# A transformer step on one core: the first scale and shift in pieces of one feature tile, products of zeros in TensorE's waits, and the last sums in another order

## The chip, the core and the metric

The kernel runs on one core of a Trainium2 chip. Its engines take their instructions in the order in which they are written: TensorE (PE; its weight loads are shown as PEld), VectorE (DVE), ScalarE (ACT), GpSimd (POOL) and SyncE (SP), which issues the transfers. The metric is the device time of one execution in microseconds, the median of several runs.

## The reference

Two layers act on 128 context tokens and 256 latent tokens of 1024 features. Each layer is a SwiGLU half step, a block of three mixers (gated short convolution, neighbourhood attention, latent attention), and a second SwiGLU half step. Ahead of each, a normalised x is scaled and shifted by vectors that come from the condition through `w_ada`:

```python
mod_ctx = (jax.nn.silu(c_ctx) @ w_ada[l] + b_ada[l]).reshape(1, 1, N_MOD, D_MODEL)
mod_lat = (jax.nn.silu(c) @ w_ada[l] + b_ada[l]).reshape(-1, 1, N_MOD, D_MODEL)
h = modulate(rmsnorm(x, ng[0]), m(0), m(1))        # h * (1 + scale) + shift
x = x + 0.5 * m(2) * swiglu(h, p['w_ffn1_gate'], p['w_ffn1_up'], p['w_ffn1_down'])
y_prompt = rmsnorm(xp, final_g)
```

The first scale and shift (m(1) and m(0) of layer 0) are needed by the very first products of the kernel; the last `rmsnorm` is its end.

## The kernel before

**Layout.** All 384 tokens lie together, features on partitions: X is eight feature tiles of 128 x 384. Every dense product is three TensorE products, since operand and weight are split into hi and lo parts: hi x hi, lo x hi, hi x lo (`mm3`). The weights come in the order of their use as chunks of 512 KB (`wst`), each eight blocks of 128 x 128. A dense chunk lands in one of three buffers raw; ScalarE writes its hi (line 320), VectorE its lo (line 321), and then the buffer is free for the next chunk (`Weights.split`, `release`, `pump`). The text calls the dense chunks d0, d1, d2 and so on. All these transfers are issued by SP, in the order of the program; one that needs a buffer waits on SP for it, and all behind it wait too. SP also waits for the transfer issued eight before.

**The start.** `first_group` makes six output tiles at once (three of the gate, three of the up projection of FFN 1), over the feature tiles k = 0 to 7; per k six groups (j = 0 to 5) of three products of 386 columns, with 48 blocks, chunks d0 to d5. The first scale and shift are not ready then. Sixteen chunks s0 to s15 of `w_ada` bring them, four at a time for a quarter of the features (two tiles). `start_quarter` multiplies the condition cz with a chunk (products of 256 columns in four column groups of the array), VectorE copies the partial sums (line 402), and `finish` transposes them and adds the four parts (lines 407, 408), adds the bias and then `scales` and `scaled` (lines 506 to 518) write hh and hl, the scaled X of the two tiles. `add_square` collects the squares of X; once all are there, 1/rms is computed by three newton steps on VectorE over 128 x 384 (`inverse_rms`, lines 432 to 451), into rb. The outputs of the first group are multiplied by rb afterwards; for all later products the eight tiles are normalised properly (`norm_tile`: line 524 on VectorE, 527 and 367 on ScalarE, 368 on VectorE), a few steps of it after each k as the table START_STEPS says.

**What follows.** `pair(f)`, f = 3 to 21, makes the other gate and up tiles (line 661), sixteen blocks each: k = 0 to 3 from one chunk, k = 4 to 7 from the next. pair(3) uses d6 and d7. The rest of the kernel is dense products one behind the other.

**The end.** X is transposed back (line 1008), the squares are summed by products with a column of ones (`rms_sums`, line 462): acc holds the tiles 0 to 6, w the last one. Three newton steps follow on VectorE, and then the scaling and the three last transfers.

Of the kernel before, what the change touches and what calls it, by code (L numbers as in the profile page):

```python
# [49 lines left out]
START_STEPS = {4: (0, 1, 0, 2, 1, 0), 5: (3, 2, 1, 4, 3, 2), 6: (5, 4, 3, 6, 5, 4), 7: (7, 6, 5, 7, 6, 7)}  # L50


START = {0: 0, 1: 1, 3: 2, 5: 3}
# [9 lines left out]
def plan():  # L63
# [3 lines left out]
    items = [("ahead", 1)]  # L67
# [11 lines left out]
    def ffn(l, n):  # L79
        g, u, dn = (f"w_ffn{1 + n // 2}_{x}" for x in ("gate", "up", "down"))  # L80
        start = (l, n) == (0, 0)
        for k in range(KD):
            if start and k in START:
                items.extend(("s", 0, m, START[k], i) for m in (1, 0) for i in range(2))
            for f in range(GROUP // 2):
                blk(g, l, k, slice(f * P, f * P + P))
                blk(u, l, k, slice(f * P, f * P + P))
# [111 lines left out]
def pack(inputs):  # L199
    order = chunks()  # L200
    out = np.empty((len(order), P, BPC * P), np.float32)
    for i, c in enumerate(order):
# [3 lines left out]
        elif c[0] == "s":  # L206
            at = c[2] * D + c[3] * 2 * P
            w = inputs["w_ada"][c[1], c[4] * D // 2:(c[4] + 1) * D // 2, at:at + 2 * P]
            out[i].reshape(P, 4, 2 * P)[:] = w.reshape(4, P, 2 * P).transpose(1, 0, 2)
# [66 lines left out]
class Weights:  # L276
# [3 lines left out]
    def __init__(self, nc, pool, src):  # L280
# [10 lines left out]
        self.ahead = 1  # L291
# [53 lines left out]
def step_kernel(ctx, tc, xT, cc, wst, cst_d, vec_d, rpb, ck_na, cv_na, ck_kv, ck_r, yd, o_k, o_v, o_ckv, o_kr):  # L345
# [36 lines left out]
    mods = [base.tile([P, NMOD, KD, 2], F32, name=f"mod{l}") for l in range(L)]  # L382
    hh = base.tile([P, KD, TOK + 2], F32R, name="hh")
# [7 lines left out]
    def start_quarter(m, c, cz):  # L391

        acc = ps()
        for half in range(2):
            i, what, raw = W.ada()
            assert what == ("s", 0, m, c, half), (what, m, c, half)
            w = raw.rearrange("p (k n) -> p k n", k=4)
            for j in range(4):
                nc.tensor.matmul(acc[32 * j:32 * j + 32, 0:2 * P], cz[:, 4 * half + j, :], w[:, j, :],
                                 start=half == 0, stop=half == 1)  # L400
        t = wt(2 * P)
        nc.vector.tensor_copy(t, acc[:, 0:2 * P])

        def finish():
            tp = ps()
            for i in range(2):
                nc.tensor.transpose(tp[:, i * P:(i + 1) * P], t[:, i * P:(i + 1) * P], ident)
            nc.vector.tensor_reduce(mods[0][:, m, 2 * c:2 * c + 2, :],
                                    tp[:, 0:2 * P].rearrange("p (i j v) -> p i v j", i=2, j=4)[:, :, 0:2, :],
                                    axis=AX.X, op=ALU.add)  # L410
            add_bias(0, m, 2 * c, 2)
# [646 lines left out]
```

## Time and profile before

| | |
|---|---|
| median of 3 runs | 1905.04 us (1904.65 to 1905.15) |
| profiled execution | 1904.49 us, its span 1902.7 us |
| TensorE busy | 1875.3 us, 99% of the span |
| VectorE, ScalarE busy | 1312.3 us, 813.2 us |
| transfers | 306.12 MB, mean 161 GB/s |

The span is the time from the first to the last instruction that the profiler saw. Times in the rows below count from the span's start. A row of a timeline merges equal instructions that follow one another and gives how many; what stands in brackets is the idle time of the engine before them, and the event that ended it.

### The profile page before, as it was taken

Reading aid. Unit: us, or ns where it says so; the run is one execution under the profiler, and the core shown is the slowest. Engines: PE = TensorE matmul, PEld = TensorE weight load, DVE = VectorE, ACT = ScalarE, POOL = GpSimd, SP = SyncE. Lnnn points to the kernel's source line nnn. Section 1 sums busy time; section 2 is a strip of 40 time slices with the busy share of each in tenths; the row PEclk is TensorE's granted clock in tenths of the full one; section 3 lists DMA queues with packets and bytes.
Section 4 is the critical chain, followed back from the end, with each engine's and each line's share of the span. In section 5 each row is a group of like instructions: output and inputs, shape, how many; then the busy total and the mean of one; then the engine's idle time right before and its main releaser. Section 6 shows DMA issues by size and latency. Waiting matters only on the chain.

```text
span 1902.7 us, 27717 instructions
## 1 busy us (share of the span) xinstructions
PE 1875.3 (99%) x10804; PEld 1824.2 (96%) x10804; DVE 1312.3 (69%) x2235; ACT 813.2 (43%) x1358; POOL 45.1 (2%) x79
## 2 busy tenths in 40 slices
PE   6999999999999999999999999999999999999998
PEld 5999999988999999999999999998789999999997
DVE  6788767665877778776778776666578766744433
ACT  4633334655533354333354333356554334633332
POOL 0000000013000000000000000000220000000000
PEclk9999999999999999999999999999999999999999
DMA  7567554423455535655535664533335643343331
GB/s 304 190 230 227 198 178 151 130 79 111 144 191 174 196 106 181 219 198 188 178 122 195 206 207 169 186 108 118 101 100 175 205 163 122 112 140 122 127 125 63
DMA packets 85523, 306.12 MB, mean 161 GB/s; under 512 B 9616, under 2 KB 11248, under 8 KB 85264
## 3 DMA queue, kind: packets, MB, share of 16 engines
q1 hardware_dynamic: 83376, 297.21, 46.8%
q0 software_dynamic: 1728, 5.41, 1.0%
q8 instruction: 84, 1.38, 0.3%
q10 hardware_dynamic: 288, 1.74, 0.3%
q14 instruction: 47, 0.39, 0.1%
HBM read 301.53 MB, written 2.79 MB: 160 GB/s over the span
## 4 chain that ended last, share of the span: by engine, by line
PE 93%; DVE 3%; ACT 2%; issue 1%; DMA 0%; SPq 0%; DVEq 0%; ACTq 0%
PE ps L661 34%; PE ps L363 18%; PE ps L362 18%; PE ps L364 18%; PE ps L874 1%; PE ps L911 1%; PE ps L927 1%; PE ps L820 1%; PE ps L818 1%; PE ps L819 1%; ACT w L527 1%; ACT prob L895 0%; DVE lo L321 0%; DVE small L889 0%; ACT hi L320 0%
## 5 line engine op out<-in xcount | busy, mean ns | idle before, releaser
L321 DVE TENSOR_TENSOR lo<-raw,hi 128x1024 fp32r<-128x1024 f32 x414 | 504.8, 1223 | 245.6 <-ACT hi L320 243.9
L320 ACT CAST hi<-raw 128x1024 fp32r<-128x1024 f32 x414 | 429.7, 1046 | 361.6 <-PE ps L363 230.8
L362 PE MATMUL ps<-hh,hi 128*128 128x384 f32 (+1 forms) x960 | 327.4, 341 | 1.9 <-ACT hh L516 1.4
L363 PE MATMUL ps<-hl,hi 128*128 128x384 f32 (+1 forms) x960 | 326.5, 340 | 2.4 <-DVE hl L368 1.8
L364 PE MATMUL ps<-hh,lo 128*128 128x384 f32 (+1 forms) x960 | 325.9, 339 | 0.0
L424 DVE SCALAR_TENSOR_TENSOR junk<-rawa,cb 128x1024 bf16<-128x1024 f32 x256 | 312.9, 1222 | 4.4
L661 PE MATMUL ps<-hl,hi 128*128 128x384 f32 x1216 | 312.6, 338 | 0.0
L661 PE MATMUL ps<-hh,lo 128*128 128x384 f32 x1216 | 312.1, 338 | 0.0
L661 PE MATMUL ps<-hh,hi 128*128 128x384 f32 x1216 | 310.3, 336 | 0.0
L364 PE MATMUL ps<-ah,lo 128*128 128x384 f32 x704 | 237.8, 338 | 0.0
L362 PE MATMUL ps<-ah,hi 128*128 128x384 f32 x704 | 237.8, 338 | 0.0
L363 PE MATMUL ps<-al,hi 128*128 128x384 f32 x704 | 237.8, 338 | 0.0
L661 PEld LDWEIGHTS ps<-hh,lo 128*128 128x128 f32 x1216 | 221.7, 188 | 0.0
L661 PEld LDWEIGHTS ps<-hh,hi 128*128 128x128 f32 x1216 | 221.3, 188 | 0.0
L661 PEld LDWEIGHTS ps<-hl,hi 128*128 128x128 f32 x1216 | 220.1, 188 | 0.0
L362 PEld LDWEIGHTS ps<-hh,hi 128*128 128x128 f32 x960 | 182.2, 190 | 5.5 <-ACT hh L516 1.8
L363 PEld LDWEIGHTS ps<-hl,hi 128*128 128x128 f32 x960 | 181.7, 189 | 3.6 <-DVE hl L368 2.3
L364 PEld LDWEIGHTS ps<-hh,lo 128*128 128x128 f32 x960 | 182.1, 190 | 0.0
L362 PEld LDWEIGHTS ps<-ah,hi 128*128 128x128 f32 x704 | 132.2, 188 | 0.0
L364 PEld LDWEIGHTS ps<-ah,lo 128*128 128x128 f32 x704 | 132.2, 188 | 0.0
L363 PEld LDWEIGHTS ps<-al,hi 128*128 128x128 f32 x704 | 132.2, 188 | 0.0
L638 ACT ACTIVATE w<-ps 128x384 f32<-128x384 f32 x76 | 37.2, 490 | 165.4 <-PE ps L661 165.4
(193 smaller groups left out, 1909.1 us busy)
## 6 DMA issues: line engine op xcount, KB each, us to landing
raw<-wst SPq DMA_DIRECT2D x414, 512.0 KB, 3.4
rawa<-wst SPq DMA_DIRECT2D x128, 512.0 KB, 3.4
s<-wst SPq DMA_DIRECT2D x16, 512.0 KB, 10.0
bias<-rpb POOLq DMA_DIRECT2D x16, 256.0 KB, 3.3
X<-xT SPq DMA_DIRECT2D x4, 384.0 KB, 9.5
y<-X SPq DMA_DIRECT2D x3, 512.0 KB, 3.9
cb<-cc ACTq DMA_DIRECT2D x1, 1024.0 KB, 6.8
cst<-cst ACTq DMA_DIRECT2D x1, 672.0 KB, 4.8
```

Source lines behind the costliest of these rows:

```text
L320: nc.scalar.copy(hi, raw)
L321: nc.vector.tensor_tensor(lo, raw, hi.bitcast(F32), op=ALU.subtract)
L362: nc.tensor.matmul(out, w[0], x[0], start=start, stop=False)
L363: nc.tensor.matmul(out, w[0], x[1], start=False, stop=False)
L364: nc.tensor.matmul(out, w[1], x[0], start=False, stop=stop)
L424: nc.vector.scalar_tensor_tensor(junk, w, 1.0, cb[:, v], op0=ALU.mult, op1=ALU.mult, accum_out=mods[l][:, m, t, v:v + 1])
L527: nc.scalar.activation(h[:, sl], h[:, sl], AF.Identity, bias=mods[l][:, 3 * idx, t, s:s + 1], scale=A[0][:, t, s:s + 1])
L638: nc.scalar.activation(s, g[:, :TOK], AF.Silu)
L661: nc.tensor.matmul(o[:, :TOK], w[part], y, start=k == 0 and i == 0, stop=k == KD - 1 and i == 2)
L818: nc.tensor.matmul(o, xh, wh, start=k == 0, stop=False)
L819: nc.tensor.matmul(o, xl, wh, start=False, stop=False)
L820: nc.tensor.matmul(o, xh, wl, start=False, stop=k == KD - 1)
```

## The change

It touches the first 60 us and the last 15 us of the kernel.

- The first scale and shift come in pieces of one feature tile. A chunk s now holds all 1024 rows of one tile's 128 columns, for scale or for shift; tile 0 needs s0 and s1, tile 1 s2 and s3, and then two tiles at a time (START). `start_tiles` takes the place of `start_quarter`: eight products of 128 columns for each chunk in place of four of 256.
- X is loaded in pieces: tile 0 behind s1, tile 1 at (k=0, j=2), tiles 2-3 at (k=1, j=0), the others at k=2. Before, two tiles each stood among the first chunks.
- At the start only one dense chunk is split ahead of tile 0's scale (`ahead` 0), the second behind tile 1's.
- `busy(n)` issues n products of a zero matrix, 128 x 512 in bf16: ten at the very start, four behind the products of s0 and s1, six behind tile 0's transposes, four behind the products of s2 and s3.
- The steps of `norm_tile` start at k=5 in place of k=4.
- At the end two tiles are transposed in place of four ahead of the sums, the three sums of acc stand ahead of those of w, and the two are added on VectorE.

```diff
--- before.py
+++ after.py
@@ -47,10 +47,12 @@
 STEPS = {2: (0, 1, 0, 2, 1, 0), 3: (3, 2, 1, 4, 3, 2), 4: (5, 4, 3, 6, 5, 4), 5: (7, 6, 5, 7), 6: (6,), 7: (7,)}
-START_STEPS = {4: (0, 1, 0, 2, 1, 0), 5: (3, 2, 1, 4, 3, 2), 6: (5, 4, 3, 6, 5, 4), 7: (7, 6, 5, 7, 6, 7)}
-START = {0: 0, 1: 1, 3: 2, 5: 3}
+START_STEPS = {5: (0, 1, 0, 2, 1, 0, 3), 6: (2, 1, 4, 3, 2, 5, 4, 3, 6), 7: (5, 4, 7, 6, 5, 7, 6, 7)}
+START = {(0, 0): ((0,), (0, 0)), (0, 2): ((1,), (0, 5)), (1, 0): ((2, 3), (1, 2)), (3, 0): ((4, 5), (3, 2)),
+         (5, 0): ((6, 7), (5, 2))}
 O_B, O_C, O_X = 0, 512, 1024
@@ -64,7 +66,7 @@
-    items = [("ahead", 1)]
+    items = [("ahead", 0)]
     def blk(name, l, k, cols):
         items.append(("d", name, l, k * P, cols))
@@ -80,9 +82,11 @@
         g, u, dn = (f"w_ffn{1 + n // 2}_{x}" for x in ("gate", "up", "down"))
         start = (l, n) == (0, 0)
         for k in range(KD):
-            if start and k in START:
-                items.extend(("s", 0, m, START[k], i) for m in (1, 0) for i in range(2))
             for f in range(GROUP // 2):
+                if start and (k, 2 * f) in START:
+                    items.extend(("s", 0, m, t) for t in START[k, 2 * f][0] for m in (1, 0))
+                    if f:
+                        items.append(("ahead", 1))
                 blk(g, l, k, slice(f * P, f * P + P))
                 blk(u, l, k, slice(f * P, f * P + P))
         if start:
@@ -204,9 +208,9 @@
             at = c[2] * D + c[3] * P
             out[i] = inputs["w_ada"][c[1], :, at:at + P].T
         elif c[0] == "s":
-            at = c[2] * D + c[3] * 2 * P
-            w = inputs["w_ada"][c[1], c[4] * D // 2:(c[4] + 1) * D // 2, at:at + 2 * P]
-            out[i].reshape(P, 4, 2 * P)[:] = w.reshape(4, P, 2 * P).transpose(1, 0, 2)
+            at = c[2] * D + c[3] * P
+            w = inputs["w_ada"][c[1], :, at:at + P]
+            out[i].reshape(P, KD, P)[:] = w.reshape(KD, P, P).transpose(1, 0, 2)
         else:
             for b, (_, name, l, r, cols) in enumerate(c[1]):
                 out[i, :, b * P:(b + 1) * P] = inputs[name][l][r:r + P, cols]
@@ -288,7 +292,7 @@
         self.parts = {}
         self.split_at = 0
         self.n = 0
-        self.ahead = 1
+        self.ahead = 0
     def pump(self, tag, upto=None):
         ring = self.rings[tag]
@@ -380,6 +384,7 @@
     nc.gpsimd.memset(up, 0.0)
     mods = [base.tile([P, NMOD, KD, 2], F32, name=f"mod{l}") for l in range(L)]
+    spool = []
     hh = base.tile([P, KD, TOK + 2], F32R, name="hh")
     hl = base.tile([P, KD, TOK + 2], F32R, name="hl")
@@ -388,27 +393,31 @@
         mod = mods[l][:, m, t:t + n, :]
         nc.vector.tensor_tensor(mod, mod, b.unsqueeze(2).to_broadcast([P, n, 2]), op=ALU.add)
-    def start_quarter(m, c, cz):
-        acc = ps()
-        for half in range(2):
-            i, what, raw = W.ada()
-            assert what == ("s", 0, m, c, half), (what, m, c, half)
-            w = raw.rearrange("p (k n) -> p k n", k=4)
-            for j in range(4):
-                nc.tensor.matmul(acc[32 * j:32 * j + 32, 0:2 * P], cz[:, 4 * half + j, :], w[:, j, :],
-                                 start=half == 0, stop=half == 1)
-        t = wt(2 * P)
-        nc.vector.tensor_copy(t, acc[:, 0:2 * P])
+    def start_tiles(ts, cz):
+        acc, n = ps(), len(ts)
+        for a, t in enumerate(ts):
+            for m in (1, 0):
+                i, what, raw = W.ada()
+                assert what == ("s", 0, m, t), (what, m, t)
+                w = raw.rearrange("p (k n) -> p k n", k=KD)
+                at = slice((n * m + a) * P, (n * m + a + 1) * P)
+                for k in range(KD):
+                    j = k % 4
+                    nc.tensor.matmul(acc[32 * j:32 * j + 32, at], cz[:, k, :], w[:, k, :], start=k < 4, stop=k >= 4)
+        x = spool[0].tile([P, 4 * P], F32, tag="st", bufs=2, name="st")[:, :2 * n * P]
+        nc.vector.tensor_copy(x, acc[:, :2 * n * P])
         def finish():
             tp = ps()
-            for i in range(2):
-                nc.tensor.transpose(tp[:, i * P:(i + 1) * P], t[:, i * P:(i + 1) * P], ident)
-            nc.vector.tensor_reduce(mods[0][:, m, 2 * c:2 * c + 2, :],
-                                    tp[:, 0:2 * P].rearrange("p (i j v) -> p i v j", i=2, j=4)[:, :, 0:2, :],
-                                    axis=AX.X, op=ALU.add)
-            add_bias(0, m, 2 * c, 2)
+            for i in range(2 * n):
+                nc.tensor.transpose(tp[:, i * P:(i + 1) * P], x[:, i * P:(i + 1) * P], ident)
+            for m in range(2):
+                nc.vector.tensor_reduce(mods[0][:, m, ts[0]:ts[0] + n, :],
+                                        tp[:, n * m * P:n * (m + 1) * P].rearrange(
+                                            "p (i j v) -> p i v j", i=n, j=4)[:, :, 0:2, :],
+                                        axis=AX.X, op=ALU.add)
+                add_bias(0, m, ts[0], n)
         return finish
@@ -542,29 +551,53 @@
             nc.vector.memset(cz, 0.0)
             nc.scalar.activation(cz[:, :, 0:2], vec[:, V_C:V_BADA].rearrange("p (k v) -> p k v", v=2), AF.Silu)
         rest = {}
-        def start(c):
-            for finish in rest.pop(c):
-                finish()
-            scales(0, 0, slice(2 * c, 2 * c + 2))
-            if c == 0:
+        if pool:
+            spool[:] = [pool]
+            warm = pool.tile([P, 512], BF16, name="warm")
+            nc.vector.memset(warm, 0.0)
+            def busy(n):
+                o = ps()
+                for _ in range(n):
+                    nc.tensor.matmul(o, warm[:, 0:P], warm, start=True, stop=True)
+            busy(10)
+        def start(ts, finish):
+            finish()
+            n = len(ts)
+            scales(0, 0, slice(ts[0], ts[0] + n))
+            if ts[0] == 0:
                 W.split(0)
-            for t in (2 * c, 2 * c + 1):
+            for t in ts:
                 scaled(t)
-            if c < 2:
-                add_square(2 * c)
-                add_square(2 * c + 1)
+            if ts[0] < 4:
+                for t in ts:
+                    add_square(t)
         out = [ps() for _ in range(GROUP)]
         for k in range(KD):
-            if pool and k in START:
-                rest[START[k]] = [start_quarter(m, START[k], cz) for m in (1, 0)]
-                if k == 0:
-                    start(0)
+            if pool and k == 2:
+                for t in (4, 6):
+                    nc.sync.dma_start(out=X[:, t:t + 2, :], in_=xT[:, t:t + 2, :])
             for j, o in enumerate(out):
-                if pool and k % 2 and k < KD - 1 and j == 2:
-                    W.prepare()
-                    start(k // 2 + 1)
+                if pool and (k, j) in START:
+                    ts, at = START[k, j]
+                    if 0 < ts[0] < 4:
+                        nc.sync.dma_start(out=X[:, ts[0]:ts[-1] + 1, :], in_=xT[:, ts[0]:ts[-1] + 1, :])
+                    rest[at] = ts, start_tiles(ts, cz)
+                    if k == 0:
+                        busy(4)
+                if pool and (k, j) in rest:
+                    if k and k < KD - 1:
+                        W.prepare()
+                    start(*rest.pop((k, j)))
+                    if (k, j) == (0, 0):
+                        busy(6)
+                    elif k == 0:
+                        W.ahead = 1
+                        W.split(1)
                 mm3(o[:, :TOK + 2], W.next(), (hh[:, k, :], hl[:, k, :]), k == 0, k == KD - 1)
             if pool and k == 2:
                 for t in range(4, KD):
@@ -619,9 +652,8 @@
         if start:
             with tc.tile_pool(name="start", bufs=1, reuse_waits="tile") as pool:
                 W.start = [pool.tile([P, BPC * P], F32, name=f"s{i}") for i in range(16)]
-                for t, upto in ((0, 5), (2, 10), (4, 12), (6, 16)):
-                    W.pump("raw", upto)
-                    nc.sync.dma_start(out=X[:, t:t + 2, :], in_=xT[:, t:t + 2, :])
+                W.pump("raw", 2)
+                nc.sync.dma_start(out=X[:, 0, :], in_=xT[:, 0, :])
                 W.pump("raw")
                 out, rb, b = first_group(l, idx, pool)
             W.ahead = AHEAD
@@ -1007,9 +1039,17 @@
                 o = out[i][t // 4][:, t % 4 * P:t % 4 * P + P]
                 nc.tensor.transpose(o, X[:, t, i * P:(i + 1) * P], ident)
-    turn(range(4))
-    [r] = rms_sums([(sumsq, D)])
-    turn(range(4, KD))
+    turn(range(2))
+    ss = ps()
+    for n, sq in enumerate(sumsq):
+        for i in range(3):
+            nc.tensor.matmul(ss[:, 3 * n + i:3 * n + i + 1], sq[:, i * P:(i + 1) * P], ones[:, 0:1],
+                             start=True, stop=True)
+    v0, v = small(3), small(3)
+    nc.vector.tensor_scalar(v0, ss[:, 0:3], 1.0 / D, EPS, op0=ALU.mult, op1=ALU.add)
+    nc.vector.scalar_tensor_tensor(v, ss[:, 3:6], 1.0 / D, v0, op0=ALU.mult, op1=ALU.add)
+    r = rsqrt(v, 3)
+    turn(range(2, KD))
     y = X.rearrange("p t c -> p (t c)").rearrange("p (i h c) -> p i h c", i=3, h=2)
     for i in range(3):
         nc.scalar.activation(y[:, i, 0, :], out[i][0], AF.Copy, scale=r[:, i:i + 1])
```

**SP around the first pieces of X.** Names: s4_84 is chunk s4, raw_100 the first dense chunk d0, raw_103 d1, raw_110 d2, raw_163 d3. Before:

```order
L304 DMA raw_100<-wst 128x1024
L624 DMA X_64<-xT 128x768
L304 DMA raw_103<-wst 128x1024 [waits DMAHW0_49]
L304 DMA s4_84<-wst 128x1024 [waits DMAHW1_49]
L304 DMA s5_85<-wst 128x1024 [waits DMAHW2_49]
L304 DMA s6_86<-wst 128x1024 [waits DMAHW3_49]
L304 DMA s7_87<-wst 128x1024 [waits DMAHW4_49]
L624 DMA X_64<-xT 128x768 [waits DMAHW5_49]
L304 DMA raw_110<-wst 128x1024 [waits DMAHW6_49]
L624 DMA X_64<-xT 128x768 [waits DMAHW7_49]
L624 DMA X_64<-xT 128x768 [waits DMAHW0_49]
L304 DMA raw_163<-wst 128x1024 [waits DMAHW1_49,DVE_49]
```

After, from d3 on (raw_172 is d3, raw_252 d4; ahead of it stand vec, cst, s0, s1, X tile 0, d0, s2, s3, d1, s4 to s7 and d2):

```order
L308 DMA raw_172<-wst 128x1024 [waits DMAHW6_49,DVE_49]
L308 DMA s8_88<-wst 128x1024 [waits DMAHW7_49]
L308 DMA s9_89<-wst 128x1024 [waits DMAHW0_49]
L308 DMA s10_90<-wst 128x1024 [waits DMAHW1_49]
L308 DMA s11_91<-wst 128x1024 [waits DMAHW2_49]
L588 DMA X_64<-xT 128x384 [waits DMAHW3_49]
L308 DMA raw_252<-wst 128x1024 [waits DMAHW4_49,DVE_49]
L308 DMA s12_92<-wst 128x1024 [waits DMAHW5_49]
L308 DMA s13_93<-wst 128x1024 [waits DMAHW6_49]
L308 DMA s14_94<-wst 128x1024 [waits DMAHW7_49]
L308 DMA s15_95<-wst 128x1024 [waits DMAHW0_49]
L588 DMA X_64<-xT 128x768 [waits DMAHW1_49]
```

X tile 1 (128x384) and X tiles 2-3 (128x768) moved behind s11 and s15; before, all of X stood ahead of s8. d4 stands between the two pieces.

**VectorE around the second dense chunk.** lo_183 and lo_249 are the lo part of d1. Before:

```order
L518 SCALAR_TENSOR_TENSOR hl_74<-X_64,A_155,hh_73 128x128
L518 SCALAR_TENSOR_TENSOR hl_74<-X_64,A_155,hh_73 128x256
L518 SCALAR_TENSOR_TENSOR hl_74<-X_64,A_155,hh_73 128x128
L518 SCALAR_TENSOR_TENSOR hl_74<-X_64,A_155,hh_73 128x256
L497 TENSOR_TENSOR acc_177<-acc_177,w_179 128x384
L321 TENSOR_TENSOR lo_183<-raw_103,hi_182 128x1024
```

VectorE after, at the same chunk; the two hl are those of tile 1:

```order
L527 SCALAR_TENSOR_TENSOR hl_74<-X_64,A_164,hh_73 128x128
L527 SCALAR_TENSOR_TENSOR hl_74<-X_64,A_164,hh_73 128x256
L506 TENSOR_TENSOR acc_182<-acc_182,w_245 128x384
L325 TENSOR_TENSOR lo_249<-raw_103,hi_248 128x1024
L409 COPY st_295<-ps_262 128x512
L325 TENSOR_TENSOR lo_304<-raw_109,hi_303 128x1024
```

d1's lo stood behind hl and the squares of the tiles 0 and 1, and stands now behind those of tile 1, whose X is a transfer of its own.

**VectorE behind the newton steps.** rb is 1/rms; w_426, w_428 and w_432 are the first three products of X with it, the copies bring the partial sums of s12 to s15. Before:

```order
L437 SCALAR_TENSOR_TENSOR rb_389<-w_388,rb_389 128x384
L321 TENSOR_TENSOR lo_403<-raw_186,hi_402 128x1024
L524 TENSOR_TENSOR w_426<-X_64,rb_389 128x384
L524 TENSOR_TENSOR w_428<-X_64,rb_389 128x384
L524 TENSOR_TENSOR w_432<-X_64,rb_389 128x384
L368 TENSOR_TENSOR hl_74<-w_426,hh_73 128x384
L402 COPY w_447<-ps_438 128x256
L402 COPY w_458<-ps_449 128x256
L321 TENSOR_TENSOR lo_467<-raw_242,hi_466 128x1024
```

VectorE after, from the last newton step on:

```order
L446 SCALAR_TENSOR_TENSOR rb_467<-w_466,rb_467 128x384
L325 TENSOR_TENSOR lo_481<-raw_252,hi_480 128x1024
L409 COPY st_537<-ps_504 128x512
L325 TENSOR_TENSOR lo_546<-raw_307,hi_545 128x1024
L416 TENSOR_REDUCE mod0_71<-ps_551 128x4
L394 TENSOR_TENSOR mod0_71<-mod0_71,vec_65 128x4
L416 TENSOR_REDUCE mod0_71<-ps_551 128x4
L394 TENSOR_TENSOR mod0_71<-mod0_71,vec_65 128x4
L515 SCALAR_TENSOR_TENSOR A_164<-mod0_71,vec_65 128x4
```

The products with rb moved from ahead of the copy to behind d5's lo (lo_546), the reduction and the hl of tiles 6 and 7.

## Rows read from the trace of the kernel before

**Rows 1.** The page's chain of what ended last: shares of the span by engine.

```profile
PE 93%; DVE 3%; ACT 2%; issue 1%; DMA 0%; SPq 0%; DVEq 0%; ACTq 0%
```

**Rows 2.** Windows: stretch, length, busy time by engine, granted clock, transfers' share, GB/s.

```profile
38.00:40.00 2.00, 2.00 (x29) 1.31 (x31) 1.87 (x4) 0.00 (x0) 0.00 (x0) 1.00 0.01 2
44.00:46.00 2.00, 0.00 (x0) 0.00 (x0) 0.89 (x2) 1.96 (x5) 0.00 (x0) 0.93 0.71 236
52.00:54.00 2.00, 2.00 (x11) 2.00 (x11) 1.56 (x3) 2.00 (x5) 0.00 (x0) 0.86 0.00 0
```

**Rows 3.** Timeline of TensorE: start, us, line, operation, count, idle before and releaser.

```profile
8.59 1.08 PE L399 MATMUL ps<-s,cz 128*32 128x256 f32 x8 [0.20 <-DMA s<-wst]
9.87 1.08 PE L399 MATMUL ps<-s,cz 128*32 128x256 f32 x8 [0.20 <-DMA s<-wst]
...
19.65 1.93 PE L399 MATMUL ps<-s,cz 128*32 128x256 f32 x32
...
22.68 0.60 PE L407 MATMUL ps<-cst,w 128*128 128x128 f32 x4
...
25.23 0.34 PE L362 MATMUL ps<-hh,hi 128*128 128x386 f32 x1
...
47.29 1.12 PE L407 MATMUL ps<-cst,w 128*128 128x128 f32 x4 [5.36 <-DVE w L402]
...
58.65 0.51 PE L661 MATMUL ps<-hh,hi 128*128 128x384 f32 x2
...
62.84 0.34 PE L661 MATMUL ps<-hh,hi 128*128 128x384 f32 x1
```

**Rows 4.** Timeline of ScalarE.

```profile
20.78 1.05 ACT L320 CAST hi<-raw 128x1024 fp32r<-128x1024 f32 x1 [4.82 <-DMA raw<-wst]
23.88 1.50 ACT L516 ACTIVATE hh<-X,A 128x128 fp32r<-128x128 f32 x4 [2.06 <-DVE A L506]
25.28 0.93 ACT L493 ACTIVATE w<-X 128x384 f32<-128x384 f32 x2
...
56.14 0.99 ACT L527 ACTIVATE w<-w,mod,A 128x128 f32<-128x128 f32 x2 [0.46 <-DVE w L524]
...
57.44 0.99 ACT L527 ACTIVATE w<-w,mod,A 128x128 f32<-128x128 f32 x2
```

**Rows 5.** Transfers of the first 60 us: queue with packets and MB; issues, us to landing.

```profile
q1 hardware_dynamic: 4778, 16.11, 69.7%
...
vec<-vec SPq DMA_DIRECT2D x1, 127.0 KB, 2.1
```

**Rows 6.** Tile raw in the first 60 us.

```profile
DMA to landing us min/median/max: 3.1/9.0/10.3
```

**Rows 7.** Timeline of VectorE.

```profile
35.67 0.56 DVE L451 TENSOR_SCALAR w<-ps 128x384 f32<-128x384 f32 x1
...
42.27 1.22 DVE L321 TENSOR_TENSOR lo<-raw,hi 128x1024 fp32r<-128x1024 f32 x1
...
46.82 0.75 DVE L402 COPY w<-ps 128x256 f32<-128x256 f32 x2
...
48.61 0.17 DVE L408 TENSOR_REDUCE mod<-ps 128x4 f32<-128x16 f32 x1
...
51.30 0.55 DVE L524 TENSOR_TENSOR w<-X,rb 128x384 f32<-128x384 f32 x1
```

**Rows 8.** Timeline of TensorE's weight loads, then of its products.

```profile
19.65 1.45 PEld L399 LDWEIGHTS ps<-s,cz 128*32 128x32 f32 x32 [0.25 <-issue]
...
49.17 0.53 PE L362 MATMUL ps<-hh,hi 128*128 128x386 f32 x1
49.49 0.52 PE L363 MATMUL ps<-hl,hi 128*128 128x386 f32 x1
```

**Rows 9.** Timeline of TensorE at the kernel's end.

```profile
1890.85 0.38 PE L462 MATMUL ps<-cst,w 128*128 128x1 f32 x2
...
1891.99 1.51 PE L1008 MATMUL ps<-cst,X 128*128 128x128 f32 x12
```

## The prediction

> **What bounds the kernel now.** I read the page's chain of waits first. TensorE holds 93% of it [rows 1], so a change elsewhere gains only where TensorE waits or runs at its lower clock. The windows of two microseconds then show where that is: nearly all in the first 60 us, the part that the change rewrites. By 38 us no transfer is left to move, and between 44 and 54 TensorE is idle or below its full clock [rows 2].
>
> The timeline of TensorE gives the marks. Two consecutive 512 KB chunks s let it start at 8.59 and 9.87, so a chunk takes 1.28 us. Step k=2 of the first six tiles (the loop over feature tiles) starts at 25.23. At 47.29 there is the one large stall, 5.36 us, until VectorE has copied a partial sum. The next stage, pair(3), starts at 58.65, and its fifth step, the first that needs weight chunk d7, at 62.84 [rows 3].
>
> Transfers land in the order of issue. Call 512 KB one unit. Between s3 (9.87) and d2, before ScalarE's wait ends at 20.78 [rows 4], SP issued d0, X tiles 0-1 (0.75 units), d1, s4 to s7, X tiles 2-3 (0.75) and d2: 8.5 units, 8.5 x 1.28 = 10.9 us, so 20.77 by the rule. All these transfers go through one queue [rows 5], with a median of 9.0 us from issue to landing [rows 6]: each waits for what was issued ahead of it.
>
> **The change part by part.**
>
> *The start, k=0.* Tile 0 alone needs s0 and s1 (landing near 6.0 and 7.3, two chunks before s3) in place of four chunks, so the first products can begin some 2.5 us earlier. I give this nothing, because the next step waits far longer, as follows.
>
> *Tile 1 of X.* In the new order of SP, X tile 1 stands behind s0, s1, X tile 0, d0, s2, s3, d1, s4 to s7, d2, d3 and s8 to s11. With vec and cst (0.5) that is 17.25 units up to its end; s3 was the end of 4.5 before. It lands at 9.87 + 12.75 x 1.28 = 26.2; before, tiles 0 and 1 landed together at 9.87 + 1.75 x 1.28 = 12.1. TensorE has its k=0 products and the products of s4 to s7 done by about 21.6 and then has nothing but k=1.
>
> Here the Trainium skill speaks against me: "DMA: Bandwidth & Descriptors", section "Queues, rings and completion order", says that completion is "not FIFO per issuing engine". If a 192 KB piece could overtake by that, X tile 1 would land shortly after its issue, and the sum would be that of the first rival below. The trace agrees with the order of issue to a hundredth of a microsecond over the 8.5 units above.
>
> *SP is held.* The next transfer, d4, reuses the buffer of d1, and waits for VectorE's lo of d1. That instruction now stands behind hl of tile 1, and ScalarE's hi of d1 behind hh and the square of tile 1. So all of them wait for X tile 1, and behind d4 on SP queue s12 to s15, X tiles 2-3, d5 and the other X tiles. From 26.2: two hh pieces 0.75 (half of 1.50), square 0.47 (half of 0.93), hi 1.05 [rows 4], lo 1.2 [rows 7] make 29.7. The queue has run dry by then, so d4 takes at least the 3.1 us of the shortest landing [rows 6]: 32.8. Four chunks s (5.1) and X tiles 2-3 (0.96) follow: 38.9. With hh (0.75) and a launch, k=2 starts at 39.8, where it was 25.23: 14.6 us later.
>
> *From k=2 to the newton steps.* TensorE has idled over 4 us by then. After the idle stretch of before, the clock was still full in most of 44 to 46 us (mean 0.93: it fell near 45.7, 3.8 us after TensorE fell idle at 41.9), and was full again at about 52.3 (mean 0.86 in 52 to 54) [rows 2], 5.0 us after the restart. A product of 386 columns starts every 0.32 us at the lower clock [rows 8]; at the full one 24 products of 384 take 62.84 - 58.65 = 4.19, 0.175 each [rows 3]. Eighteen products are then 15 x 0.32 + 3 x 0.18 = 5.3 us: 45.1. The s products of a pair of tiles are now 64 records of 128 columns in place of 32 of 256, which took 1.93 us [rows 3]. If columns set their time, they stay at 1.93; if each record does (0.06), 3.86. I take 2.9: the weight loads of before kept 0.045 a record [rows 8], and this lies about in the middle. So 48.0. The page "TensorE: Matmul & The Clock Gate" of the Trainium skill (section "Wait — 56ns, not 53.3ns?") puts a floor of about 25 ns under a small product; 64 of them would be 1.6, an estimate by which the total would be 1.3 us lower, and no run shows it yet. Then two groups of three products (1.05) and four transposes (0.60) [rows 3]: 49.7; and VectorE's chain from the reduction to the last hl, 48.61 to 51.30 = 2.7 [rows 7]: 52.4, and 0.2 for the products of the squares' sums that also precede: 52.6. The newton steps start there, in place of 35.67.
>
> *From newton to the next stage.* Newton takes 35.67 to 42.27, 6.6 us: 59.2. Before, lo, three products with rb and ScalarE's first norm tile stood between it and the copy that TensorE awaited, 42.27 to 46.82; now lo of d4 (1.2) and the copy (0.75) alone [rows 7]. So the stall of 5.36 shrinks: the transposes start at 61.2. But all eight norm tiles now come behind lo of d5 (1.2), 2.7 from reduction to hl, and 0.65 for the first product with rb (0.55) and a launch: 59.2 + 1.2 + 0.75 + 1.2 + 2.7 + 0.65 = 65.7. Each tile costs ScalarE 1.30 (56.14 to 57.44) [rows 4], with hi of d6 (1.05) among them: 65.7 + 10.4 + 1.05 = 77.2. Only behind these stand hi of d7 (1.05) and lo of d7 (1.2): 79.4. TensorE meanwhile does transposes (0.6), four groups at k=5 (2.1), twelve at k=6 and 7 (6.3): pair(3) starts at 70.2, its four steps with d6 (4.2) end at 74.4, and it waits 5.0 us for d7. Its fifth step starts at 79.4 in place of 62.84: 16.6 us later. This is the term that counts; the 14.6 above lies inside it. After it TensorE is the bound again and nothing returns the time.
>
> *The clock there.* 5.0 us of idling exceed the 3.8 after which the clock fell before. If it falls, some 16 products (5.0 us at 0.32) cost 0.145 more each, 2.3; if not, 0. I take the fall: 2.3, and keep both ends.
>
> *Products of zeros.* Ten, four, six and four of them, 512 bf16 columns each; no row has one. By the nearest row, 386 columns in 0.32 at the lower clock, one takes 0.42, and ten run from about 1.5 to 5.7 us, just within the wait for s0. If a column cost four times that, they would hold the first chunk by 12 us, still inside the wait for X tile 1, which hides the other fourteen as well; what they could gain, a full clock from the first product, ends in the same wait. So 0, either way.
>
> *The last sums.* Before, three sums of w alternate with three of acc and the first of w waits until w is squared: five from 1890.85 to 1891.99, 0.23 each [rows 9]. Now three of acc stand ahead, and three of w follow it, 0.69: 0.45 less on the path to the newton steps of the end. Eighteen transposes in place of twelve stand behind them, at 0.15 each (0.60 for four [rows 3]) 0.9 more, which those steps cover or nearly. So -0.5; bounds -1 and +0.5.
>
> **The sum.** 16.6 + 2.3 - 0.5 = +18.4 on the profiled execution's 1904.5: 1922.9. That execution lies 0.5 below the median of the three runs, 1905.0; I forecast 1923. A chain of this length is no surer than 2 us, and the fall of the clock is worth 2.3, so this case alone spans 1918.5 to 1925.
>
> **The rivals.** *Small transfers overtake.* Then X tile 1 lands some 2.1 us after its issue at 16.8 (behind s6's landing), as vec did [rows 5]; SP is let go at about 22.7, before the queue is dry, X tiles 2-3 land near 28, and k=2 starts at 28.7. Newton starts at 28.7 + 3.2 + 2.9 + 1.8 + 2.7 = 39.3, and the fifth step of pair(3) comes 26.8 later as above: 66.1, 3.3 late; less 0.5, 1907.3. That is not slower by what can be told: 0.2%, 3.8 us, is about the least that a measurement of this kernel tells from no change. It decides if X tile 1 lands by 20. For it speaks that no transfer of 192 KB is in the trace; against it the landing of d2.
>
> *The late chunk is covered.* If VectorE and ScalarE got to d7 before TensorE needs it, only the later start of pair(3) would stay: 70.2 - 58.65 = 11.6, less 0.5: 1915.6. The norm tiles would have to run at 0.7 us each; against it speaks 1.30 on ScalarE, where the order leaves no gap.
>
> *More goes cold.* If the transposes in the middle keep the clock low through k=2 and k=3, and every s product is at its upper bound, newton starts 3 to 5 us later still: 1927.
>
> **Chances.** Forecast 0.70; more goes cold 0.12; late chunk covered 0.10; overtaking 0.05; something unseen that leaves a gain 0.03. Faster 0.03, within 0.2% 0.05, slower 0.92. The range 1916 to 1927 leaves out the overtaking, the gain and a part of the ends.
>
> **What would show it.** Right: no transfer moves between about 27 and 31 us; TensorE idle some 5 us before k=1, and 4 to 6 before k=2; newton from 52 to 59; hi of d7 behind the last norm tile and TensorE idle in pair(3) until about 79. Wrong: X tile 1's hh on ScalarE before 20 us, or d7's lo done before 75.

## The result and the profile after

The changed kernel takes 1922.01 us (median of 4 runs, 1921.79 to 1923.59), against 1904.85 for the kernel before on the same chip (4 runs): a ratio of 1.0093, 95% interval 1.0075 to 1.011. The forecast was 1923, slower. The profiled execution took 1921.79, its span is 1920.0. Lines of the new kernel stand up to 40 further down: 366 to 368 are `mm3`, 407 the products of s, 409 the copy, 414 the transposes, 525 and 527 hh and hl, 693 the products of `pair`.

The page's chain of waits, shares by engine, then the first of those by line:

```profile
PE 91%; DVE 3%; ACT 2%; DMA 2%; issue 1%; SPq 0%; DVEq 0%; ACTq 0%
PE ps L693 33%; PE ps L366 17%; PE ps L367 17%; PE ps L368 17%; PE ps L906 1%; PE ps L943 1%; DMA X<-xT 1%; PE ps L959 1%; ACT w L536 1%; DMA s<-wst 1%; PE ps L852 1%; PE ps L850 1%; PE ps L851 1%; DVE lo L325 1%; ACT hi L324 0%
```

Transfers hold 2% where they held 0 [rows 1], and X stands among them by name. The timeline of TensorE (answers to [rows 3]):

```profile
11.39 0.45 PE L366 MATMUL ps<-hh,hi 128*128 128x386 f32 x1 [1.35 <-ACT hh L525]
...
17.98 1.96 PE L407 MATMUL ps<-s,cz 128*32 128x128 f32 x64
...
28.05 0.69 PE L366 MATMUL ps<-hh,hi 128*128 128x386 f32 x1 [8.11 <-ACT hh L525]
...
42.56 0.69 PE L366 MATMUL ps<-hh,hi 128*128 128x386 f32 x1 [6.57 <-ACT hh L525]
...
62.49 0.78 PE L414 MATMUL ps<-cst,st 128*128 128x128 f32 x4 [2.56 <-DVE st L409]
...
73.04 0.51 PE L693 MATMUL ps<-hh,hi 128*128 128x384 f32 x2
...
79.32 0.61 PE L693 MATMUL ps<-hh,hi 128*128 128x384 f32 x2 [1.92 <-ACT hi L324]
...
80.58 1.01 PE L693 MATMUL ps<-hh,lo 128*128 128x384 f32 x2
```

The start is earlier and then two new waits stand, 8.11 us for X tile 1 (k=1) and 6.57 for tiles 2-3 (k=2). The old wait of 5.36 has become one of 2.56, and pair(3) has a new one, 1.92, for chunk d7.

ScalarE and SP show what TensorE waits for ([rows 4]; the issues are SP's):

```profile
17.27 0.33 SPq L588 DMA_DIRECT2D X<-xT  x1
30.63 0.33 SPq L308 DMA_DIRECT2D raw<-wst  x1
31.00 1.87 SPq L308 DMA_DIRECT2D s<-wst  x4
32.91 0.44 SPq L588 DMA_DIRECT2D X<-xT  x1
```

```profile
27.20 0.80 ACT L525 ACTIVATE hh<-X,A 128x128 fp32r<-128x128 f32 x2 [15.45 <-DMA X<-xT]
...
28.32 1.98 ACT L324 CAST hi<-raw 128x1024 fp32r<-128x1024 f32 x2
...
41.71 1.49 ACT L525 ACTIVATE hh<-X,A 128x128 fp32r<-128x128 f32 x4 [11.41 <-DMA X<-xT]
...
78.23 2.94 ACT L324 CAST hi<-raw 128x1024 fp32r<-128x1024 f32 x3
```

Tile 1, issued at 17.27, is used at 27.20, 9.9 us later. SP then issues nothing until 30.63, when VectorE's lo of d1 (29.38 to 30.60) has freed a buffer: d4, and tiles 2-3 behind it. The windows show the dry queue and the clock (columns as in [rows 2]):

```profile
24.00:26.00 2.00, 0.00 (x0) 0.00 (x0) 0.00 (x0) 0.00 (x0) 0.00 (x0) 0.83 0.73 281
26.00:28.00 2.00, 0.00 (x0) 0.00 (x0) 0.35 (x1) 0.80 (x3) 0.00 (x0) 0.50 0.03 10
28.00:30.00 2.00, 1.95 (x5) 1.72 (x6) 1.59 (x3) 2.00 (x3) 0.00 (x0) 0.50 0.00 0
30.00:32.00 2.00, 1.29 (x6) 0.78 (x6) 2.00 (x3) 0.29 (x1) 0.00 (x0) 0.50 0.24 47
...
42.00:44.00 2.00, 1.44 (x4) 1.21 (x5) 1.81 (x5) 2.00 (x7) 0.00 (x0) 0.50 0.50 201
...
60.00:62.00 2.00, 0.00 (x0) 0.00 (x0) 1.97 (x4) 0.00 (x0) 0.00 (x0) 1.00 0.00 0
62.00:64.00 2.00, 1.51 (x7) 1.51 (x8) 1.93 (x6) 0.00 (x0) 0.00 (x0) 0.72 0.49 156
64.00:66.00 2.00, 2.00 (x8) 2.00 (x8) 1.69 (x8) 1.49 (x4) 0.00 (x0) 0.50 0.78 217
80.00:82.00 2.00, 1.88 (x6) 1.42 (x5) 2.00 (x3) 1.16 (x2) 0.00 (x0) 0.50 0.90 322
```

Hardly a byte moves from 26 to 30 us, the transfers' share being 0.03 and 0.00, and it is still 0.24 in the next window. The granted clock is 0.50, the lower level, in four stretches: around k=1, at k=2 (42 to 44), behind the transposes at 62.5, and in pair(3) at 80.

VectorE at d1's lo, around the newton steps, and in pair(3) (for [rows 7]):

```profile
29.38 1.22 DVE L325 TENSOR_TENSOR lo<-raw,hi 128x1024 fp32r<-128x1024 f32 x1 [0.38 <-ACT hi L324]
...
54.01 0.55 DVE L460 TENSOR_SCALAR w<-ps 128x384 f32<-128x384 f32 x1
...
61.75 0.68 DVE L409 COPY st<-ps 128x512 f32<-128x512 f32 x1
...
79.30 3.50 DVE L325 TENSOR_TENSOR lo<-raw,hi 128x1024 fp32r<-128x1024 f32 x3
```

TensorE at the end (for [rows 9]):

```profile
1907.43 0.34 PE L368 MATMUL ps<-ah,lo 128*128 128x384 f32 x1
...
1909.16 0.83 PE L1046 MATMUL ps<-cst,w 128*128 128x1 f32 x6 [0.17 <-ACT w L502]
1909.85 2.16 PE L1040 MATMUL ps<-cst,X 128*128 128x128 f32 x18
```

The last product of the kernel before:

```profile
1889.12 0.34 PE L364 MATMUL ps<-ah,lo 128*128 128x384 f32 x1
```

The last product starts 18.3 us later than before, the span is 17.3 longer.

### The profile page after: what moved, and what is told of

It is laid out like the page before. It is cut to its first block, busy times and chain, and to the rows that moved or that the text cites. A ratio compares the mean times of both kernels' runs of the same rounds, so it can differ in the third digit from the quotient of the medians.

```text
span 1920.0 us, 28027 instructions
## 1 busy us (share of the span) xinstructions
PE 1884.0 (98%) x10956; PEld 1832.3 (95%) x10956; DVE 1313.5 (68%) x2241; ACT 813.4 (42%) x1358; POOL 44.9 (2%) x79
## 4 chain that ended last, share of the span: by engine, by line
PE 91%; DVE 3%; ACT 2%; DMA 2%; issue 1%; SPq 0%; DVEq 0%; ACTq 0%
PE ps L693 33%; PE ps L366 17%; PE ps L367 17%; PE ps L368 17%; PE ps L906 1%; PE ps L943 1%; DMA X<-xT 1%; PE ps L959 1%; ACT w L536 1%; DMA s<-wst 1%; PE ps L852 1%; PE ps L850 1%; PE ps L851 1%; DVE lo L325 1%; ACT hi L324 0%
## 5 line engine op out<-in xcount | busy, mean ns | idle before, releaser
L366 PE MATMUL ps<-hh,hi 128*128 128x384 f32 (+1 forms) x960 | 328.5, 342 | 16.5 <-ACT hh L525 16.0
```

The costliest lines, as they stand in the source:

```text
L366: nc.tensor.matmul(out, w[0], x[0], start=start, stop=False)
```

## The experiments

Each is given with its median, and the ratio to the kernel before on the same chip with its 95% interval.

**X early.** The changed kernel, all of X among the first chunks again; everything else stays as changed.

```diff
-                W.pump("raw", 2)
-                nc.sync.dma_start(out=X[:, 0, :], in_=xT[:, 0, :])
+                for ts, upto in ((slice(0, 1), 2), (slice(1, 2), 3), (slice(2, 4), 10), (slice(4, 6), 11), (slice(6, 8), 11)):
+                    W.pump("raw", upto)
+                    nc.sync.dma_start(out=X[:, ts, :], in_=xT[:, ts, :])
                 W.pump("raw")
...
-            if pool and k == 2:
-                for t in (4, 6):
-                    nc.sync.dma_start(out=X[:, t:t + 2, :], in_=xT[:, t:t + 2, :])
...
-                    if 0 < ts[0] < 4:
-                        nc.sync.dma_start(out=X[:, ts[0]:ts[-1] + 1, :], in_=xT[:, ts[0]:ts[-1] + 1, :])
```

> The changed kernel with the transfers of X put back among the first chunks: tile 1 behind d0, tiles 2-3 behind s7, the others behind d2; all else as changed. Theory (X queued behind the chunks and SP held by it): no wait before k=1 and k=2 beyond 2 us, newton near 40 us, some 13 to 15 us less than the changed kernel, 1907 to 1909. Rival (the pieces of one tile, twice as many small products, the zeros or the later norm tiles cost it): little of the 17 us comes back, over 1915.

1905.49, ratio 1.0003 (0.9994 to 1.0012). 16.5 of the 17.2 us are gone, and the time is 1.5 under the range expected. TensorE's timeline:

```profile
25.82 0.44 PE L366 MATMUL ps<-hh,hi 128*128 128x386 f32 x1 [0.96 <-ACT hh L525]
...
45.72 0.66 PE L414 MATMUL ps<-cst,st 128*128 128x128 f32 x4 [2.54 <-DVE st L409]
...
62.55 0.61 PE L689 MATMUL ps<-hh,hi 128*128 128x384 f32 x2 [1.93 <-ACT hi L324]
```

k=2 is back at 25.8, and the wait in pair(3) has stayed: it belongs to the order of the norm tiles, not to late X.

**Which piece of X.** Four kernels. First tile 1 and tiles 2-3 through ScalarE's own queue, at the same places (tiles 4 to 7 stay on SP):

```diff
-                        nc.sync.dma_start(out=X[:, ts[0]:ts[-1] + 1, :], in_=xT[:, ts[0]:ts[-1] + 1, :])
+                        nc.scalar.dma_start(out=X[:, ts[0]:ts[-1] + 1, :], in_=xT[:, ts[0]:ts[-1] + 1, :])
```

> The changed kernel with the same two transfers (X tile 1, X tiles 2-3) at the same places of the program, issued by ScalarE on its own queue in place of SP's. Theory (a transfer waits for what its own queue was given before): tile 1 lands before 18 us and tiles 2-3 before 27, no long wait before k=1; X tiles 4 to 7 stay on SP and hold the squares, so 6 to 10 us less than the changed kernel, 1912 to 1916. Rival (the transfer engines serve all requests in the order of issue): tile 1 lands near 26 us still, within 2 us of 1922.

1914.99, 1.0056 (1.0041 to 1.0071), as expected. The two transfers, with the us from issue to landing at the end of each row:

```profile
X<-xT ACTq DMA_DIRECT2D x1, 192.0 KB, 6.9
X<-xT ACTq DMA_DIRECT2D x1, 384.0 KB, 6.2
```

Issued at 10.70 and 18.63, they land at 17.6 and 24.8. Tile 1 lands ahead of s7, which SP had issued before it and for which TensorE waits until 20.73: on a queue of their own these transfers overtake the chunks. (ScalarE also issues tile 1 earlier than SP did, at 10.70 in place of 17.27.) Then the kernel before with one part, its tiles 2-3 and 4 to 7 issued at k=1 and k=2:

```diff
-                for t, upto in ((0, 5), (2, 10), (4, 12), (6, 16)):
+                for t, upto in ((0, 5),):
...
+            if pool and k in (1, 2):
+                for t in ((2,) if k == 1 else (4, 6)):
+                    nc.sync.dma_start(out=X[:, t:t + 2, :], in_=xT[:, t:t + 2, :])
```

> The kernel before with one part alone: transfers of feature tiles 2-3 are issued at the first group's step 1 and of 4 to 7 at step 2, as in the changed kernel, behind the chunks on SyncE's queue; pieces, products, steps and last sums stay as before. Theory (a feature tile issued behind the chunks lands as late as the queue ahead of it is long): k=2 of the first group starts at 33 to 36 us instead of 25.2, a good part of it is lost to the end, 1911 to 1914. Rival (the smaller pieces, the new order of the products or the zeros carry the loss): 1905 to 1907.

1915.78, 1.0057 (1.0044 to 1.0069): 10.9 lost, and k=2 at 35.25 as expected; the time is 1.8 over the range.

```profile
35.25 0.69 PE L362 MATMUL ps<-hh,hi 128*128 128x386 f32 x1 [10.56 <-ACT hh L516]
```

Last, the changed kernel with only tile 1 early, and with only tiles 2-3 early; the first of them:

```diff
+                for ts, upto in ((slice(0, 1), 2), (slice(1, 2), 3)):
+                    W.pump("raw", upto)
+                    nc.sync.dma_start(out=X[:, ts, :], in_=xT[:, ts, :])
...
-                    if 0 < ts[0] < 4:
+                    if ts[0] == 2:
```

and the second, with two lines other than that:

```diff
+                for ts, upto in ((slice(0, 1), 2), (slice(2, 4), 10)):
...
+                    if ts[0] == 1:
```

> The changed kernel with X tile 1 alone issued early (behind d0); tiles 2-3 and 4 to 7 stay where the change put them. My step 'SP is held': d4 waits for the split of d1, which stands behind tile 1, so late tile 1 also delays tiles 2-3. If so, with tile 1 early SP isn't held, X tiles 2-3 land in line, 5.75 units of 1.28 us behind s11 (26 to 27), at 33.5 to 34.5, k=2 starts near 35 in place of 42.6, and the time is 1913.5 to 1916.5. Rival (SP's hold costs nothing, the queue alone sets tiles 2-3): they land at 41 again and the time stays at 1920 or more.

> The changed kernel with X tiles 2-3 alone issued early (behind s7, before d2); tile 1 and tiles 4 to 7 stay late. Then k=1 starts at 28 to 29.5 as in the changed kernel, k=2 follows it at 36 to 37 without a wait, the newton steps start at 46 to 48 in place of 54, and the time is 1914 to 1917. Rival (the late tile 1 is the whole loss, since SP is held by it): 1920 or more; the other (tile 1's wait is hidden behind what k=2 waits for): under 1910.

Tile 1 early: 1915.46, 1.0054 (1.0039 to 1.0069), as expected. Tiles 2-3 early: 1921.81, 1.0088 (1.0071 to 1.0105), a miss; nothing is won. ScalarE with tile 1 early, and then TensorE and ScalarE with tiles 2-3 early:

```profile
34.67 1.49 ACT L525 ACTIVATE hh<-X,A 128x128 fp32r<-128x128 f32 x4 [12.78 <-DMA X<-xT]
```

```profile
49.09 1.11 PE L414 MATMUL ps<-cst,st 128*128 128x128 f32 x4 [5.85 <-DVE st L409]
```

```profile
44.20 1.89 ACT L502 ACTIVATE w<-X 128x384 f32<-128x384 f32 x4 [6.20 <-DMA X<-xT]
```

With tile 1 early, d4 isn't held (SP issues it at 21.55) and tiles 2-3 are there at 34.67 in place of 41.71. With tiles 2-3 early, the wait before k=2 is gone, but tiles 4 to 7 still stand behind the held d4; their squares come at 44.20, VectorE adds them ahead of the copy of the partial sums, and TensorE waits 5.85 us for that. The newton steps start at 54.05, as in the changed kernel (54.01). So the late tile 1, with the hold on SP that it causes, costs 6.5 us of the 17 (1922.0 less 1915.5), and whichever pieces of X stand behind the hold last carry the loss on. The hold by itself, with tile 1 still late, was not tried.

**The products of zeros.** All four groups left out.

```diff
             def busy(n):
-                o = ps()
-                for _ in range(n):
-                    nc.tensor.matmul(o, warm[:, 0:P], warm, start=True, stop=True)
+                pass
```

> The changed kernel without the products of zeros. Theory: they end in the wait for X tile 1 and move nothing behind it: 1921 to 1923; only the first products run at the lower clock. Rival (they hold up s0's products and the transposes): 1 us or more less. Other rival (they keep the clock up where it counts): 1 us or more longer.

1923.22, 1.0098 (1.0081 to 1.0115): 0.2 over the range expected, and 1.2 more than the changed kernel, which taken alone would speak for the second rival. But the runs of the two kernels overlap (1921.79 to 1923.59, and 1922.46 to 1923.98 here), and the marks hardly differ: k=2 starts at 42.04 for 42.56, the fifth step of pair(3) at 79.40 for 79.32. The zeros move nothing that can be told from the spread; a gain of about 1 us by them is not ruled out.

**The table of steps.** The changed kernel with the table of before.

```diff
-START_STEPS = {5: (0, 1, 0, 2, 1, 0, 3), 6: (2, 1, 4, 3, 2, 5, 4, 3, 6), 7: (5, 4, 7, 6, 5, 7, 6, 7)}
+START_STEPS = {4: (0, 1, 0, 2, 1, 0), 5: (3, 2, 1, 4, 3, 2), 6: (5, 4, 3, 6, 5, 4), 7: (7, 6, 5, 7, 6, 7)}
```

> The changed kernel with the table of steps of the kernel before (six steps of normalised tiles at k=4, 5 and 6 each and six at k=7, instead of seven, nine and eight at k=5, 6 and 7). Theory (the late feature tiles carry the loss, and the tiles of the norm wait for the root in either order): 1921 to 1923, as the changed kernel. Rival (the later steps are part of the loss, as the fourth pair starts 2.8 us later than forecast): 1917 to 1920.

1921.96, 1.0087 (1.0074 to 1.0101). TensorE's only wait between k=3 and 110 us:

```profile
65.91 1.12 PE L414 MATMUL ps<-cst,st 128*128 128x128 f32 x4 [5.96 <-DVE st L409]
```

The table only moves a wait: with the old one it is 5.96 at the transposes, with the new 2.56 there and 1.92 at d7. A stretch at the lower clock follows each of them.

**Chunk d7 early.** The changed kernel, d7 split ahead of most norm tiles.

```diff
+            if pool and k == 6:
+                W.ahead = 2
```

> The changed kernel with one line more: at k=6 the split of weights is let run two chunks ahead, so that hi and lo of d7 stand before most of the norm tiles. Theory (pair(3) waits for d7 behind the norm tiles, and the clock falls in that wait): TensorE no longer idles 2 us near 78 us and keeps the full clock there, 2.5 to 4 us less, 1918 to 1919.5. Rival (the wait is for the norm tiles themselves or for PSUM): within 0.7 us of 1922.

1921.19, 1.0087 (1.0072 to 1.0102): 0.8 less than the changed kernel where 2.5 to 4 were expected. The wait for d7 is gone and this one has come four steps later, at pair(4):

```profile
82.84 0.88 PE L695 MATMUL ps<-hh,hi 128*128 128x384 f32 x2 [1.63 <-DVE w L678]
```

VectorE frees the PSUM of the first group by two multiplications, and they stand behind its lo of d8 and d9 (79.86, 2.36 us). The profile is that of the fastest of the four runs (1919.74 to 1923.23), and the clock stays at 1.00 behind the wait in it. The same edit with X early, then with a lead of one chunk in pair(3), and of two (the cut shows the last; the one before it starts from a lead of 1 and gains one in each pair):

> The changed kernel with the feature tiles issued early (as in the run that gave 1905.5) and with chunk 7 split into its two parts ahead of most of the normalised tiles. There the fifth step of the fourth pair waited 1.93 us and the clock stood at half for some 4 us behind it. Theory (the wait goes and the next one, for PSUM behind VectorE's two later splits, takes some of it): 1904.0 to 1905.0. Rival (both waits cost all alike): 1905.5.

> As the run before it, but after the first group the splits keep one chunk of lead, and gain one per pair, so that VectorE frees the PSUM of the first two products of the group ahead of the splits of chunks 8 and 9. Theory: neither wait is left, the 1.93 us and about 2 us of half clock come back: 1902.0 to 1903.5, under the kernel before. Rival (a lead of one leaves the next chunk late, and TensorE waits at pair 4's or 5's start): 1905 or more.

```diff
-            W.ahead = AHEAD
+            W.ahead = 2
...
                     if k == 3 and group:
                         group.pop(0)()
+                    if start and k == 3 and f > GROUP // 2:
+                        W.ahead = AHEAD
```

> As the run with feature tiles and chunk 7 early (1903.9), with a lead of two chunks in pair 3 and three from pair 4 on: the split of chunk 8 stays ahead of the two multiplications that free PSUM, that of chunk 9 goes behind them. There pair 4 waited 1.63 us for them, behind two splits of 1.18 us on VectorE, and the clock stood at half for some 4 us after it. Theory: the wait falls to 0.3 to 0.6 us and the clock stays up, 1901.0 to 1902.5, under the kernel before by a gain that can be measured. Rival (the wait only moves again, to chunk 9 or later): 1904 or more.

1903.93, 0.9995 (0.9987 to 1.0004); 1906.83, 1.001 (1.0001 to 1.0019); 1903.98, 0.9995 (0.9986 to 1.0004). A lead of one is too short, as the rival had it: the wait is for hi of d8, 2.16 us. A lead of two leaves 0.56, but the time is that of the first, above the range expected. One reason is in its trace: four times between 59 and 63 us TensorE's weight loads wait 0.22 to 0.29 us, 1.1 in all, for VectorE's hl of the norm tiles. None of these beats the kernel before by what can be told. TensorE at pair(4) in the last:

```profile
65.70 0.88 PE L691 MATMUL ps<-hh,hi 128*128 128x384 f32 x2 [0.56 <-DVE w L674]
```

**The last sums alone.** The kernel before with only the new tail.

```diff
-    turn(range(4))
-    [r] = rms_sums([(sumsq, D)])
-    turn(range(4, KD))
+    turn(range(2))
+    ss = ps()
...
+    r = rsqrt(v, 3)
+    turn(range(2, KD))
```

> The kernel before with only the new order of the last sums (two feature tiles turned ahead of the sums instead of four, the sums of both squares in one PSUM tile and added by VectorE). My theory priced it at -0.5; in the changed kernel the stretch from the last product to the end was 1.0 us shorter than before (12.57 against 13.58), so now I expect 1904.0 to 1904.4, a gain of 0.6 to 1.0. Rival, that the last stretch was shorter there only by chance of one profile: 1905.0, no change.

1904.63, 0.9997 (0.9988 to 1.0006): 0.2 less, no change that can be told. From the last product to the issue of the outputs it takes 6.38 us (1889.55 to 1895.93), against 6.63 before. The changed kernel's profile shows 1.0 less from the last product to the end, 0.55 of it ahead of that issue and the rest in the landing of the outputs.

## Why the prediction was right, step by step

The verdict and the mechanism held: late X, not the smaller pieces, makes the kernel slower, which the run with X early shows. That the total of 1922.9 came within 1 us of the 1922.0 measured is partly luck: steps that were off cancelled.

- *X tile 1* was to land at 26.2 and is used at 27.20. TensorE waited 8.11 us for it and not "some 5", since the products of s4 to s7 were done at 19.9 and not at 21.6. The transfers ran at the 410 GB/s of the forecast (512 KB in 1.28 us) but for a stretch near the start, and the last bytes came slowly (0.03 at 26 to 28, above). Windows of either kind:

```profile
6.00:8.00 2.00, 1.45 (x34) 0.74 (x24) 0.37 (x1) 0.00 (x0) 0.00 (x0) 1.00 1.02 308
...
22.00:24.00 2.00, 0.00 (x0) 0.00 (x0) 0.00 (x0) 0.00 (x0) 0.00 (x0) 1.00 1.03 412
```

- *The rival* by which small transfers overtake fell: tile 1 is used at 27.20 and not by 20. The run with ScalarE's queue, where the two pieces did overtake, comes nearest to it, and gave 1915 and not 1907, since tiles 4 to 7, still on SP, were late. The rival's 1907 has no term for them.
- *SP is held* was right: d4 at 30.63 for 29.7, late by what tile 1 was late. The run with tile 1 early shows d4 at 21.55, without the hold.
- *Tiles 2-3* came 11.1 us after d4's issue, not 9.2, and k=2 at 42.56, not 39.8. The step that failed is "Four chunks s (5.1) and X tiles 2-3 (0.96) follow", by 1.28 us for each chunk. The rows give the us from issue to landing of s12 (issued at 31.00), s13 (about 31.5) and tiles 2-3 (32.91):

```profile
s<-wst SPq DMA_DIRECT2D x1, 512.0 KB, 4.2
...
s<-wst SPq DMA_DIRECT2D x1, 512.0 KB, 6.6
...
X<-xT SPq DMA_DIRECT2D x1, 384.0 KB, 8.7
```

  So s12 landed at 35.2, s13 only at 38.1, and tiles 2-3 at 41.6. From s12 to s13 it took 2.9 us in place of 1.28, 1.6 of the 1.9 lost. SP had d5 and tiles 4 to 7 issued by 35.3, and bytes of transfers issued later moved meanwhile: 12 us at 327 GB/s are 3.9 MB, where d4, four chunks and tiles 2-3 make 3.0.

```profile
30.00:42.00 12.00, 5.28 (x18) 4.46 (x17) 3.32 (x10) 0.58 (x2) 0.00 (x0) 0.64 0.87 327
```

  The landings stayed in the order of issue here too, so this is not the rule that the prediction weighed and set aside, "not FIFO per issuing engine" (the Trainium skill, "DMA: Bandwidth & Descriptors", section "Queues, rings and completion order"). That the sharing with later transfers is the cause, and not another delay, was not tried by itself.
- *The products of s* for a pair of tiles took 1.96, where I took 2.9 between bounds of 1.93 and 3.86: the lower bound, columns set the time, 0.031 for 128 of them. (The estimate from the floor that the Trainium skill's page "TensorE: Matmul & The Clock Gate" gives, section "Wait — 56ns, not 53.3ns?", was 1.6, 0.36 too low; as a floor it is not contradicted.)
- *Newton* started at 54.01, forecast 52.6. Of the 2.8 us lost at k=2, half was got back: 0.9 by those products and 0.3 by the eighteen of k=2, which took 5.0 for 5.3, since the clock was full again from about 45.8 on.
- *The stall at the transposes* shrank as said, 5.36 to 2.56, from 59.9. But it ended 1.3 later than forecast, and the clock fell behind it, which I had only at pair(3): 0.50 at 64 to 66. So pair(3) started at 73.04 and not 70.2.
- *The wait for d7* was therefore 1.92 in place of 5.0, and yet the fifth step came at 79.32 for 79.4: ScalarE's norm tiles at 1.30 each set it, whatever TensorE does meanwhile. Two errors cancel in the last 0.1: the norm tiles ended at 78.2 and not 77.2, and the step waits for hi of d7 (79.2) and not for lo, as I had put it. Only its products with lo wait for that, until 80.58.
- *The clock* did fall there (0.50 at 80 to 82), though TensorE had waited 1.92 and not 5.0. My reason, an idle stretch longer than 3.8, was not met, so that this term came out is luck. From the fifth step, 16.5 late, to the last product, 18.3 late, 1.8 more were lost, a part of it to the wait for lo; I took 2.3.
- *Zeros* 0: not contradicted, since 1.2 lies within the spread. *The last sums* -0.5: 0.25 by the run alone, and too small to be told.

Sum measured on the profiled executions: 16.5 + 1.8 = 18.3 at the last product, less 1.0 behind it, 17.3; the forecast was 16.6 + 2.3 - 0.5 = 18.4.

## What to carry to other kernels

In this kernel a small transfer put behind big ones on one queue landed as late as all of them (192 KB 9.8 us after its issue); and where its consumer stands, on an in-order engine, ahead of the work that frees a buffer, the queue itself then stops, and everything behind it is late too (no issue from 17.27 to 30.63 us here). Such losses do not add up piece by piece: with tiles 2-3 alone moved back, the others carried the whole delay (1921.8), so the whole row has to be walked until the last waiter is named. Where a wait goes, price the next one on the same engine before counting the gain: d7's 1.92 us turned into 1.63 at PSUM.

## What the runs showed of the hardware

The same stall, 2.5 us at the transposes, left the clock in two ways. The windows of the kernel with X early, and of the one with a lead of two:

```profile
46.00:48.00 2.00, 2.00 (x11) 2.00 (x10) 1.70 (x8) 0.41 (x2) 0.00 (x0) 0.60 0.81 260
48.00:50.00 2.00, 2.00 (x8) 2.00 (x8) 1.93 (x6) 1.08 (x3) 0.00 (x0) 0.55 0.77 250
```

```profile
46.00:48.00 2.00, 1.91 (x13) 1.91 (x14) 1.90 (x8) 0.04 (x1) 0.00 (x0) 1.00 0.70 233
48.00:50.00 2.00, 1.92 (x10) 1.38 (x10) 1.73 (x7) 1.46 (x4) 0.00 (x0) 1.00 0.69 193
```

TensorE waited 2.54 us in both (to 45.72, to 46.09); in the first the clock went to its lower level soon after, in the second it stayed at 1.00. The wait of 1.63 us at pair(4) did the same: 1.00 behind it with d7 early alone, 0.66 from 68 to 72 us with X early as well. What decides it no run here tells. A product of 512 bf16 columns of zeros took about 0.40 us in the first group (10 in 3.99), at the start, and 0.26 in the next (4 in 1.04), though the windows show a granted clock of 1.00 for both.
